# Storing one of eight expert results between two pieces of the last weight load

## The chip, the cores and the metric

The kernel runs on one core of a Trainium2 chip. A core has TensorE for matmuls, VectorE and ScalarE for elementwise work, GpSimd and SyncE, and 16 DMA engines that move data between the chip's memory (HBM) and the on-chip memory (SBUF). Engines run side by side and wait for one another through semaphores. A transfer is issued by one of the engines into its queue; the 16 DMA engines then serve the queues, and the transfer raises a semaphore by 16 when all of it has landed. The metric is the device time of one execution in microseconds (us).

## The reference

Eight experts, each with two layers and a ReLU between them:

```python
# x: [8, 256, 512], w1: [8, 512, 2048], w2: [8, 2048, 512], float32
h = np.matmul(x, w1)
h = np.maximum(h, 0)
return np.matmul(h, w2).astype(np.float32)     # [8, 256, 512]
```

Per expert 512 KB of x, 4 MB of w1 and 4 MB of w2 come in, and 512 KB of result go out. All the weights are read once: 64 MB in float32.

## The kernel before

**Where the data lies.** Weights are converted to bf16 by the transfer that loads them, so 4 MB in HBM become 2 MB in SBUF. There are two buffers for w1 and two for w2; expert e uses buffer e % 2. The results have a place for every expert: `o_sb` holds all eight, `[128, 8, 2, 512]` in float32, and nothing in it is overwritten.

**The computation.** Experts go in pairs, four rounds of a loop. In each round TensorE runs layer 1 of both experts (L255 to L275, 64 matmuls per expert into `ph`), while VectorE and ScalarE apply the ReLU and write `ht` (L215, L217). Then it runs layer 2 of both (L277 to L296). One expert's layer 2 is 16 contraction tiles times two halves of the rows, 32 matmuls into one PSUM tile `po`, which VectorE and ScalarE copy to `o_sb`, one half each (L224). Each copy raises a counter by one: `s_dve` for VectorE, `s_act` for ScalarE. The helper `copied(eng, n)` (L100) makes an engine wait for both counters, so for the results of the first n experts.

**What sets the order of the loads.** All weights are loaded through GpSimd's queue, in an order written out by hand (L139 to L162): the w1 of a pair, then its w2, each held back until the buffer that it fills is free. The w2 load of the last two experts is cut into two transfers, the first 9 contraction tiles (1152 KB, L136) and the other 7 (896 KB, L137), so that the pass can begin on the first piece. TensorE does not wait for loads directly: SyncE waits for each load's semaphore in turn and hands TensorE a token (`t_w`, L105 to L121). For the last expert TensorE takes one token before contraction tile 0 and one before tile 9 (L285). Before the first of them, SyncE also waits until the previous expert's result has been copied out of `po` (L116).

**The stores.** There are three before the change. GpSimd issues one for results 0 to 3 at the end of its program, after the last weight transfer (L163, L164). SyncE issues one for results 4 to 6, after it has seen the last weight piece land and result 6 copied (L122, L123), and one for result 7 when that has been copied (L124, L125). At the end SyncE waits for the three store semaphores (L298, L299).

Of the kernel before, what the change touches and what calls it, by code (L numbers as in the profile page):

```python
# [9 lines left out]
def kernel(  # L10
# [13 lines left out]
    E, C, H = x.shape  # L24
# [6 lines left out]
    G = E // 2  # L31
# [5 lines left out]
    out_r = out.rearrange("e (p mt) n -> p e mt n", p=P)  # L37
# [18 lines left out]
    o_sb = nc.alloc_sbuf_tensor("out_sb", [P, E, MT, H], f32)  # L56
# [8 lines left out]
    s_out = [sem(f"s_out{i}") for i in range(3)]  # L65
# [18 lines left out]
    sp, pool, act, dve, pe = nc.sync, nc.gpsimd, nc.scalar, nc.vector, nc.tensor  # L84
# [15 lines left out]
    def copied(eng, n):  # L100
        eng.wait_ge(s_act, n)
        eng.wait_ge(s_dve, n)
# [28 lines left out]
    def load_w2(e):  # L131
        k = e % 2 * KT2
        if e < E - 2:
            pool.dma_start(w2_k[:, k:k + KT2], w2_r[e]).then_inc(s_w2[e], 16)  # L134
        else:
            pool.dma_start(w2_k[:, k:k + CUT], w2_r[e, :, :CUT]).then_inc(s_w2[e], 16)  # L136
            pool.dma_start(w2_k[:, k + CUT:k + KT2], w2_r[e, :, CUT:]).then_inc(s_w2b[e - E], 16)  # L137

    load_x(pool, G - 1, 1, 2)  # L139
# [12 lines left out]
        channel_multiplier=1,  # L152
    ).then_inc(s_id, 1)
    load_w2(0)
    load_w2(1)
    for e in range(2, E, 2):
        for b in range(2):
            pool.wait_ge(s_first, e + b - 1)
            load_w1(e + b)
        for b in range(2):  # L160
            pool.wait_ge(s_act, e + b - 1)
            load_w2(e + b)  # L162
    copied(pool, G)  # L163
    pool.dma_start(out_r[:, :G], o_sb[:, :G]).then_inc(s_out[0], 16)  # L164
    pool.drain()


# [127 lines left out]
                    if kt == KT2 - 1:  # L295
                        ins.then_inc((s_ob, s_oa)[m], 1)  # L296

    for s in s_out:  # L298
        sp.wait_ge(s, 16)  # L299


# [28 lines left out]
```

## Time and profile before

| What | Value |
|---|---|
| Median of 3 runs | 179.64 us (179.51 to 179.72) |
| The profiled execution: time | 179.63 us |
| The profiled execution: span from first to last instruction | 178.3 us |
| TensorE busy | 134.0 us, 75% |
| VectorE, ScalarE busy | 37.1 us, 37.8 us |
| HBM read, written | 71.30 MB, 4.19 MB |
| Mean granted TensorE clock | 0.943 |

The times quoted below are in microseconds from the start of the span. In the page's slices, each digit is a tenth of the busy share of one of 40 equal slices (9 is 90% or more), and the GB/s row counts the bytes that the transfers wrote. "Landing" is the moment at which a transfer's semaphore is complete; a row of the transfers gives the size of one and the time from issue to landing. In rows of the timeline the columns are start, duration, engine, line, operation and operands, and in brackets the idle time before it with what ended it. "SPq" is SyncE's queue of instructions.

### The profile page before, as it was taken

The page shows a single profiled execution, that of the slowest core. Times are in us where ns is not written, and L with a number is a line of the kernel's source. Part 1 is how long each engine was busy: PE and PEld are TensorE (multiplying, and loading weights), DVE is VectorE, ACT ScalarE, POOL GpSimd, SP SyncE. Part 2 cuts the span into 40 slices and gives each one's busy share as a digit, 9 for nine tenths or more (in the row PEclk, how much of TensorE's full clock was granted, in tenths as well). Part 3 has the DMA queues.
Part 4 walks back from the last instruction along what each step waited for, and adds up shares of the span by engine and source line. Part 5 has one row for each costly group of instructions (what it writes and reads, how often), then busy time and mean ns, then how long its engine had stood idle before and what let it go on. Part 6 is the DMA issues. An engine that isn't in the chain of part 4 may idle for free. (4 is left out here: it accounts for less than half of the span.)

```text
span 178.3 us, 2361 instructions
## 1 busy us (share of the span) xinstructions
PE 134.0 (75%) x832; PEld 90.8 (51%) x832; DVE 37.1 (21%) x48; ACT 37.8 (21%) x49; POOL 12.9 (7%) x27
## 2 busy tenths in 40 slices
PE   0044479899949697899769399999499695998950
PEld 0033368796414296785233278874134694953420
DVE  0132653342010133131101023330100242311010
ACT  2455555222010122121100013230100221311010
POOL 3600000101010101001000100110200400000000
PEclk9999999999987999699999759999969999999996
DMA  6999999999999999999998999999999999999998
GB/s 210 347 211 232 232 199 217 232 206 210 235 202 210 235 210 202 235 210 202 235 221 191 235 221 195 232 232 199 217 232 202 213 235 190 214 217 210 269 422 359
DMA packets 4368, 40.90 MB, mean 229 GB/s; under 512 B 400, under 2 KB 400, under 8 KB 2192
## 3 DMA queue, kind: packets, MB, share of 16 engines
q0 software_dynamic: 3408, 37.23, 95.1%
q1 hardware_dynamic: 960, 3.67, 5.3%
HBM read 71.30 MB, written 4.19 MB: 423 GB/s over the span
## 5 line engine op out<-in xcount | busy, mean ns | idle before, releaser
L268 PE MATMUL pt_h<-xe,w_sb 128*128 x512 | 67.3, 291 | 11.2 <-PEq L87 11.1
L268 PEld LDWEIGHTS pt_h<-xe,w_sb 128*128 x512 | 58.8, 148 | 20.2 <-issue 17.1
L288 PE MATMUL pt_o<-w_sb,ht_sb 128*128 x256 | 59.9, 395 | 8.9 <-PEq L87 8.8
L288 PEld LDWEIGHTS pt_o<-w_sb,ht_sb 128*128 x256 | 25.5, 101 | 41.8 <-issue 15.6
L217 DVE TENSOR_SCALAR ht_sb<-pt_h 128x512 bf16<-128x512 f32 x32 | 22.1, 692 | 52.3 <-PE pt_h L268 52.3
L215 ACT ACTIVATE ht_sb<-pt_h 128x512 bf16<-128x512 f32 x32 | 19.1, 597 | 57.3 <-PE pt_h L268 57.3
L252 PE MATMUL pt_tr<-identity,x_b 128*128 128x128 bf16 x64 | 7.5, 308 | 17.8 <-PEq L87 17.8
L224 DVE COPY out_sb<-pt_o 128x512 f32 x8 | 5.5, 692 | 65.4 <-PE pt_o L288 65.4
L224 ACT COPY out_sb<-pt_o 128x512 f32 x8 | 4.7, 585 | 63.6 <-PE pt_o L288 63.6
L252 PEld LDWEIGHTS pt_tr<-identity,x_b 128*128 128x128 bf16 x64 | 6.5, 142 | 18.5 <-issue 18.5
L129 POOL DMA_DIRECT2D w_sb<-in_w_dram x8 | 5.0, 625 | 73.3 <-ACTq L219 73.3
L194 DVE COPY xe<-pt_tr 128x1024 bf16<-128x1024 bf16 x2 | 4.9, 2460 | 5.2 <-PE pt_tr L252 5.2
L194 ACT COPY xe<-pt_tr 128x1024 bf16<-128x1024 bf16 x2 | 4.9, 2455 | 4.1 <-PE pt_tr L252 4.1
L134 POOL DMA_DIRECT2D w_sb<-in_w_dram x6 | 3.2, 536 | 34.0 <-ACT out_sb L224 33.9
L175 ACT CAST x_b<-x_f 128x1024 bf16<-128x1024 f32 x2 | 4.0, 1986 | 3.2 <-DMA x_f<-in_x_dram 3.2
L191 DVE COPY xe<-pt_tr 128x1024 bf16<-128x1024 bf16 x2 | 1.4, 692 | 8.1 <-PE pt_tr L252 8.1
L175 DVE CAST x_b<-x_f 128x1024 bf16<-128x1024 f32 x2 | 2.1, 1060 | 4.2 <-DMA x_f<-in_x_dram 4.2
L191 ACT COPY xe<-pt_tr 128x1024 bf16<-128x1024 bf16 x2 | 2.0, 1012 | 4.1 <-PE pt_tr L252 4.1
L136 POOL DMA_DIRECT2D w_sb<-in_w_dram x2 | 1.1, 528 | 17.6 <-ACT out_sb L224 17.6
L175 ACT COPY x_b<-x_c 128x1024 bf16<-128x1024 bf16 x2 | 2.2, 1122 | 0.0
L175 ACT ACT_TABLE_LOAD x1 | 1.3, 1283 | 2.5 <-PEq L98 2.5
L175 DVE COPY x_b<-x_c 128x1024 bf16<-128x1024 bf16 x2 | 1.4, 698 | 0.0
(10 smaller groups left out, 4.0 us busy)
## 6 DMA issues: line engine op xcount, KB each, us to landing
w_sb<-in_w_dram POOLq DMA_DIRECT2D x14, 2048.0 KB, 28.8
w_sb<-in_w_dram POOLq DMA_DIRECT2D x2, 1152.0 KB, 25.5
out_dram<-out_sb POOLq DMA_DIRECT2D x1, 2048.0 KB, 34.0
w_sb<-in_w_dram POOLq DMA_DIRECT2D x2, 896.0 KB, 29.4
out_dram<-out_sb SPq DMA_DIRECT2D x1, 1536.0 KB, 8.6
x_f<-in_x_dram SPq DMA_DIRECT2D x1, 1024.0 KB, 5.7
x_c<-in_x_dram POOLq DMA_DIRECT2D x1, 1024.0 KB, 9.4
x_f<-in_x_dram SPq DMA_DIRECT2D x1, 512.0 KB, 3.4
```

The costliest lines, as they stand in the source:

```text
L129: pool.dma_start(w1_k[:, e % 2 * KT1:(e % 2 + 1) * KT1], w1_r[e]).then_inc(s_w1[e], 16)
L134: pool.dma_start(w2_k[:, k:k + KT2], w2_r[e]).then_inc(s_w2[e], 16)
L136: pool.dma_start(w2_k[:, k:k + CUT], w2_r[e, :, :CUT]).then_inc(s_w2[e], 16)
L175: copy(x_b[:, b].rearrange("p (t m) q -> p t m q", m=MT), src.rearrange("p m (q t) -> p t m q", t=KT1),).then_inc(t_xb, 1)
L191: copy(xe[:, a * n:(a + 1) * n], pt[b][:].rearrange("p j q -> p (j q)")).then_inc(s_xe[b], 1)
L194: copy(xl[:, :, :, :, a - G].rearrange("p l j q -> p j l q"), pt[b][:].rearrange("p j (l q) -> p j l q", l=G),).then_inc(s_xe[b], 1)
L215: act.activation(dst, ph[half][:], relu).then_inc(t_h, 1)
L217: dve.tensor_relu(dst, ph[half][:]).then_inc(t_h, 1)
L224: copy(outs[b], po[:, half]).then_inc(s_copied, 1)
L252: ins = pe.transpose(pt[b][:, j], x_b[:, b, j], identity[:])
L268: ins = pe.matmul(ph[i // 2][:, i % 2, :], ws[i % 2 * KT1 + kt], xs[kt], start=(kt == 0), stop=(kt == KT1 - 1),)
L288: ins = pe.matmul(po[:, m], hs[(kt - k0) * MT + m], ws[kt - k0], start=(kt == 0), stop=(kt == KT2 - 1),)
```

## The change

GpSimd issues the store of result 0 as a transfer of its own, 512 KB, after the first piece of expert 7's w2 and before the second. Ahead of it stands a wait for result 0's two copies. The store at the end of GpSimd's program now covers results 1 to 3, 1536 KB. Both raise the same semaphore, so SyncE's last wait asks for 32 on it instead of 16. Nothing else is changed.

```diff
@@ load_w2 @@
             pool.dma_start(w2_k[:, k:k + CUT], w2_r[e, :, :CUT]).then_inc(s_w2[e], 16)
+            if e == E - 1:
+                copied(pool, 1)
+                pool.dma_start(out_r[:, 0], o_sb[:, 0]).then_inc(s_out[0], 16)
             pool.dma_start(w2_k[:, k + CUT:k + KT2], w2_r[e, :, CUT:]).then_inc(s_w2b[e - E], 16)
@@ end of GpSimd's program @@
     copied(pool, G)
-    pool.dma_start(out_r[:, :G], o_sb[:, :G]).then_inc(s_out[0], 16)
+    pool.dma_start(out_r[:, 1:G], o_sb[:, 1:G]).then_inc(s_out[0], 16)
     pool.drain()
@@ SyncE's last waits @@
-    for s in s_out:
-        sp.wait_ge(s, 16)
+    for i, s in enumerate(s_out):
+        sp.wait_ge(s, 16 if i else 32)
```

## The prediction

> **What bounds the kernel now.** I read the slices of the page first, then the transfers and their landings, then the waits of SyncE, then the end of the span in small windows.
>
> ```profile
> span 178.3 us, 2361 instructions
> DMA  6999999999999999999998999999999999999998
> GB/s 210 347 211 232 232 199 217 232 206 210 235 202 210 235 210 202 235 210 202 235 221 191 235 221 195 232 232 199 217 232 202 213 235 190 214 217 210 269 422 359
> q0 software_dynamic: 3408, 37.23, 95.1%
> q1 hardware_dynamic: 960, 3.67, 5.3%
> PE 4%; ACT 0%; issue 0%
> ```
>
> The DMA row stands at 9 tenths in nearly every slice, the last ones included. The chain that ended last holds only 4% of TensorE, its last layer-2 pass; what comes after it is a transfer. The kernel is bound by bytes through the 16 DMA engines, and nearly all go through GpSimd's queue (q0, 95.1%). The rate of the row doubles at the end, from about 215 to 422 GB/s, because it counts bytes written: a weight load reads float32 and writes bf16, a store writes what it reads.
>
> Which transfer ends last, by issue time and time to landing:
>
> ```profile
> 139.11 0.53 POOL L136 DMA_DIRECT2D w_sb<-in_w_dram  x1 [10.39 <-ACT out_sb L224]
> 139.63 0.54 POOL L137 DMA_DIRECT2D w_sb<-in_w_dram  x1
> 140.15 0.76 POOL L164 DMA_DIRECT2D out_dram<-out_sb  x1
> 168.37 0.39 SPq L123 DMA_DIRECT2D out_dram<-out_sb  x1
> 172.51 0.36 SPq L125 DMA_DIRECT2D out_dram<-out_sb  x1
> ...
> w_sb<-in_w_dram POOLq DMA_DIRECT2D x1, 1152.0 KB, 24.7
> w_sb<-in_w_dram POOLq DMA_DIRECT2D x1, 896.0 KB, 28.6
> out_dram<-out_sb POOLq DMA_DIRECT2D x1, 2048.0 KB, 34.0
> out_dram<-out_sb SPq DMA_DIRECT2D x1, 1536.0 KB, 8.6
> out_dram<-out_sb SPq DMA_DIRECT2D x1, 512.0 KB, 5.7
> ```
>
> Adding the two times: the first piece of expert 7's w2 lands at 139.11 + 24.7 = 163.8, the second at 139.63 + 28.6 = 168.2, the store of results 0 to 3 at 140.15 + 34.0 = 174.2, that of 4 to 6 at 168.37 + 8.6 = 177.0 and that of 7 at 172.51 + 5.7 = 178.2. The last landing is the end of the span. GpSimd's three land in the order of issue and were all issued over 20 us before they could move, so its queue is one line, long filled ahead.
>
> The end in windows. Columns: stretch, its length, busy time of PE, PEld, DVE, ACT and POOL, granted clock, DMA share, GB/s.
>
> ```profile
> 163.00:168.23 5.23, 4.44 (x21) 1.87 (x20) 0.69 (x1) 0.58 (x1) 0.00 (x0) 1.00 1.01 217
> 168.23:177.50 9.27, 3.63 (x17) 1.47 (x15) 0.69 (x1) 0.58 (x1) 0.00 (x0) 0.87 1.02 422
> 176.00:176.50 0.50, 0.00 (x0) 0.00 (x0) 0.00 (x0) 0.00 (x0) 0.00 (x0) 0.50 1.02 418
> 176.50:177.00 0.50, 0.00 (x0) 0.00 (x0) 0.00 (x0) 0.00 (x0) 0.00 (x0) 0.50 1.02 418
> 177.50:178.00 0.50, 0.00 (x0) 0.00 (x0) 0.00 (x0) 0.00 (x0) 0.00 (x0) 0.50 0.28 107
> ```
>
> From 163 to 177.5 the engines have a share of 1: no gap between the two w2 pieces, between load and store, or where SyncE's queue alone is left (176 to 177). The bytes that remain after the second piece are 8 results of 512 KB, 4.194 MB, and 4.194 MB / 422 GB/s = 9.94 us; 168.23 + 9.94 = 178.17 against the landing at 178.2. So the end is the landing of the second w2 piece plus the stores at full rate.
>
> **The change part by part.** The sum is made against the profiled execution: 178.3 us of span, 179.63 us with what lies around it, 0.01 under the median of the runs, 179.64.
>
> Result 0 on its own. The 2048 KB store becomes one of 512 KB ahead of the second w2 piece and one of 1536 KB behind it. No byte is added. The 512 KB take 0.524 MB / 422 GB/s = 1.24 us of all engines before the second piece, and as much less after it. For the DMA engines: +1.24 and −1.24, sum 0. GpSimd issues one transfer more, 0.53 us by the row of L136, and the second piece is issued some 0.6 us later, at about 140.2. That costs nothing, since its turn on the engines comes only after 163; without that cover it would be 0.6 us.
>
> The new wait on GpSimd, for expert 0's two output copies. Behind it stand the second piece and the other store. It is already met:
>
> ```profile
> L224 DVE COPY out_sb<-pt_o x8: 691/692/692, 49.2 to 171.7; 128x512 f32 x8
> L224 ACT COPY out_sb<-pt_o x8: 585/585/586, 49.4 to 171.9; 128x512 f32 x8
> ```
>
> The first copies start at 49.2 and 49.4 and take 0.7 and 0.6 us, so both counts are there by 50, and GpSimd comes to the wait at about 139.6, after the issue of the first piece. Cost 0.
>
> The second w2 piece lands 1.24 us later, at 168.23 + 1.24 = 169.47. TensorE waits for it before its contraction tile 9 of 16, that is after 18 of 32 matmuls:
>
> ```profile
> SPq L121 <- DMA w_sb<-in_w_dram: 3.6, 1, 3.6
> L121 SPq EVENT_SEMAPHORE  x2: 17/17/17, 158.4 to 168.2; - x2
> 164.80 7.07 PE L288 MATMUL pt_o<-w_sb,ht_sb 128*128 x32 [0.79 <-PEq L87]
> 171.69 0.69 DVE L224 COPY out_sb<-pt_o 128x512 f32 x1 [7.16 <-PE pt_o L288]
> 171.90 0.58 ACT L224 COPY out_sb<-pt_o 128x512 f32 x1 [7.27 <-PE pt_o L288]
> ```
>
> SyncE passes that wait at 168.2 and hands the token on. TensorE reaches tile 9 at 164.80 + 18 x 7.07 / 32 = 168.78 and does not stop: the pass is one run of 32. The slack is 0.5 us, and the delay of 1.24 us uses it up. I expect a new stall of 1.24 − 0.5 = 0.7 us, 0.9 if SyncE's handing-on takes 0.2. The copies then end at 172.48 + 0.8 = 173.3, and the store of result 7 is issued at 173.4 instead of 172.51.
>
> What is queued behind SyncE's wait: the store of results 4 to 6. It goes from 168.37 to about 169.6, as it is issued once the second piece has landed.
>
> Does the late issue reach the end? Only if the engines run out of work first. From 169.47 there are 7 results left, 3.670 MB / 422 GB/s = 8.70 us, up to 178.17, as before. Without result 7 the others keep the engines until 178.17 − 1.24 = 176.9 by landings, and some 0.6 us earlier, 176.3, by the last byte (the data of the profiled run end in the window 177.5 to 178 at 0.28 x 0.5 = 0.14, so at 177.64, against the landing at 178.2). A transfer started from rest needs this long to its first bytes:
>
> ```profile
> 0.74 0.87 SPq L92 DMA_DIRECT2D x_f<-in_x_dram  x2
> 1.00:1.50 0.50, 0.00 (x0) 0.00 (x0) 0.00 (x0) 0.00 (x0) 0.00 (x0) 1.00 0.00 0
> 1.50:2.00 0.50, 0.00 (x0) 0.00 (x0) 0.00 (x0) 0.00 (x0) 0.00 (x0) 1.00 0.65 90
> ```
>
> Issue at 0.74, first bytes between 1.5 and 2: about 1.0 us, at most 1.3. So the store of result 7 is in time if it is issued by about 175.2; it comes at 173.4. The stall of 0.8 us is covered by 1.8 us. The first store of SyncE has the same cover: it must be ready before GpSimd's 1536 KB are through, at 169.47 − 0.6 + 1.573 MB / 422 GB/s = 172.6, and is, at 169.6 + 1.0 = 170.6. Cost of both on the path: 0. What is late next, were the stall longer, is the issue of result 7.
>
> The engines now go from load to store, back to load, and to store again. The change from load to store costs nothing that the share shows (1.01 and 1.02 on either side). The change from a store back to a load is in no row. Nearest rows: a transfer behind another on the same queue, 0, from the share of 1.02 in 176 to 177, where SyncE's second store follows its first; and a start from rest, 1.0 us. GpSimd's queue is filled ahead, which makes it the first of the two: I take 0.05 us, and keep 0 and 1.0. Below nothing it goes if the store slips in beside the load, which writes only 217 GB/s: at most the 1.24 us of the store.
>
> A term of this one execution lies in the same place:
>
> ```profile
> 165.00:165.50 0.50, 0.50 (x4) 0.25 (x3) 0.00 (x0) 0.00 (x0) 0.00 (x0) 1.00 1.19 229
> 165.50:166.00 0.50, 0.50 (x4) 0.24 (x3) 0.00 (x0) 0.00 (x0) 0.00 (x0) 1.00 1.18 172
> 166.00:166.50 0.50, 0.50 (x4) 0.20 (x2) 0.00 (x0) 0.00 (x0) 0.00 (x0) 1.00 0.70 115
> 166.50:167.00 0.50, 0.50 (x4) 0.24 (x3) 0.00 (x0) 0.00 (x0) 0.00 (x0) 1.00 0.93 186
> ```
>
> The load falls from 217 to 172, 115 and 186 GB/s for half a microsecond each, (45 + 102 + 31) x 0.5 = 89 KB, at 217 GB/s 0.4 us, from no cause that I see. If it does not come again the time falls by up to 0.4; if a store there makes it worse, it grows by as much.
>
> Sum: +1.24 − 1.24 + 0 (issue) + 0 (wait) + 0 (stall, covered) + 0.05 = +0.05, on 179.64: 179.7.
>
> **The rivals.** *Slower: the ring stands still between a store and what follows it.* If the completion mark of result 0's store holds GpSimd's queue until its last byte is confirmed in memory, the engines idle, for SyncE's queue is empty then. The price is the time from last byte to landing at the end, 178.2 − 177.64 = 0.57: 180.2. Against it stands the seamless pass from SyncE's first store to its second, 1.02; for it, that this is another queue, and that no store of GpSimd's has anything behind it yet. A read that starts cold after the store would cost about the same or up to 1.0.
>
> *Slower: a transfer more pays a whole start and end.* The rows give 1.0 for a start and 0.57 for an end: 1.57, 181.2. Against it: the two w2 pieces are two transfers already, 4.4 us apart for 896 KB, and show no hole in the share. The Trainium skill, "DMA: Bandwidth & Descriptors", section "Anatomy of one DMA — SWDGE (gpsimd) path", states a fit of about 2.0 us per transfer plus its bytes at 436 GB/s. Read as a charge on every transfer, it speaks against cutting a store in two, and the sum by it would be an estimated 181.6; the trace bears the rate out (422) and not the charge for transfers that are queued back to back.
>
> *Slower: the stall reaches the end.* This decides only if the result 7 store is issued after 175.2, the second piece landing past 171.3 in place of 169.47. It needs 1.8 us more than 512 KB cost; one more microsecond beyond that gives 180.6. GpSimd's queue would have to be served out of order, which its three landings deny.
>
> *Faster: the store hides under the load.* A load occupies half of the write side (217 against 422 GB/s). If the engines used the rest, all of result 0's 1.24 us would vanish: 178.4; a half, 179.0; the dip at 165.5 to 167 not coming again, 179.2. Against the first: the share is 1.0 in loads already, and an engine that must read 4 bytes for each 2 written has no reading side left for a store.
>
> **How the numbers follow.** Faster or slower means over 0.2%, 0.36 us, about what a measurement here tells from no change. Bytes conserved, no gap: 0.60, 179.7, its own range 179.3 to 180.0. The ring stands still or reads start cold, 180.2 to 180.6: 0.18. A full start and end: 0.06. The stall reaches the end: 0.04. Faster by overlap or by the missing dip: 0.12, mostly at 179.0 to 179.2. So faster 0.12, same 0.60, slower 0.28. The range 179.2 to 180.6 leaves out the full charge, the long stall and most of the overlap, under 2 in 10.
>
> **What would show it.** Right: the second piece lands about 1.2 us later, near 169.5; the last layer-2 pass splits into 18 and 14 matmuls with 0.7 to 0.9 us between; SyncE's stores go out near 169.6 and 173.4; the DMA share stays at 1 from 163 to 177.5; the last landing stays at 178.2. Wrong: a half-microsecond window between 163 and 170 with a share well under 1 that the trace of before does not have (the ring stands still, or the cold read); a hole after 176 (the late issue); a second piece that lands less than 0.8 us later (overlap).

## The result, and the profile after

The changed kernel takes 179.88 us against 179.59 us (medians of 20 executions each): a ratio of 1.0015 with a 95% interval of 1.0009 to 1.0022. It is slower by about 0.27 us, clearly above nothing and, at 0.15%, inside the 0.2% that was called no change, though the upper end of the interval lies just outside. It also spreads more. The executions of before lie between 179.51 and 179.91, those of the changed kernel between 179.56 and 180.55, leaving out a single one of 340.15.

The profiled execution took 179.56 us with a span of 178.2. GpSimd's and SyncE's issues in its timeline:

```profile
139.16 0.53 POOL L136 DMA_DIRECT2D w_sb<-in_w_dram  x1 [10.38 <-ACT out_sb L227]
139.71 0.54 POOL L139 DMA_DIRECT2D out_dram<-out_sb  x1
140.24 0.54 POOL L140 DMA_DIRECT2D w_sb<-in_w_dram  x1
140.77 0.76 POOL L167 DMA_DIRECT2D out_dram<-out_sb  x1
169.58 0.39 SPq L123 DMA_DIRECT2D out_dram<-out_sb  x1
173.44 0.36 SPq L125 DMA_DIRECT2D out_dram<-out_sb  x1
```

The transfers of the same execution, by size and time from issue to landing:

```profile
w_sb<-in_w_dram POOLq DMA_DIRECT2D x1, 1152.0 KB, 24.8
out_dram<-out_sb POOLq DMA_DIRECT2D x1, 512.0 KB, 25.6
w_sb<-in_w_dram POOLq DMA_DIRECT2D x1, 896.0 KB, 29.2
out_dram<-out_sb POOLq DMA_DIRECT2D x1, 1536.0 KB, 32.5
out_dram<-out_sb SPq DMA_DIRECT2D x1, 1536.0 KB, 7.4
out_dram<-out_sb SPq DMA_DIRECT2D x1, 512.0 KB, 4.8
```

The first piece lands at 139.16 + 24.8 = 164.0, result 0 at 165.3, the second piece at 140.24 + 29.2 = 169.44, results 1 to 3 at 173.3, 4 to 6 at 177.0 and 7 at 178.2. In this execution the order of the landings has changed and the end has not.

TensorE's last pass in the timeline:

```profile
164.84 3.83 PE L291 MATMUL pt_o<-w_sb,ht_sb 128*128 x17 [0.79 <-PEq L87]
169.61 3.18 PE L291 MATMUL pt_o<-w_sb,ht_sb 128*128 x14 [0.93 <-PEq L87]
```

The pass of 32 is now two runs with a stall of 0.93 us (one matmul record is missing). The DMA engines over the whole stretch, in the columns of the windows shown before:

```profile
163.00:177.50 14.50, 8.06 (x36) 3.28 (x35) 1.38 (x2) 1.17 (x2) 0.00 (x0) 1.00 1.00 350
```

The share is 1.00, where the same window of before has 1.02, and the span is 178.2 us against 178.3. So this execution shows no loss against before, and the 0.27 us of the medians must lie in others.

### The profile page after: what moved, and what is told of

It reads as the page before. It is cut to its first block, busy times and chain, and to the rows that moved or that the text cites. A ratio compares the mean times of both kernels' runs of the same rounds, so it can differ in the third digit from the quotient of the medians.

```text
span 178.2 us, 2355 instructions
## 1 busy us (share of the span) xinstructions
PE 129.4 (73%) x824; PEld 88.0 (49%) x832; DVE 37.1 (21%) x48; ACT 37.8 (21%) x49; POOL 13.4 (7%) x28
## 5 line engine op out<-in xcount | busy, mean ns | idle before, releaser
L271 PE MATMUL pt_h<-xe,w_sb 128*128 x512 | 63.2, 278 | 12.7 <-PEq L87 12.7
L291 PE MATMUL pt_o<-w_sb,ht_sb 128*128 x248 | 59.1, 394 | 13.1 <-PEq L87 12.7
L271 PEld LDWEIGHTS pt_h<-xe,w_sb 128*128 x512 | 56.3, 146 | 20.2 <-issue 19.4
```

The lines of the kernel that those rows point to most:

```text
L271: ins = pe.matmul(ph[i // 2][:, i % 2, :], ws[i % 2 * KT1 + kt], xs[kt], start=(kt == 0), stop=(kt == KT1 - 1),)
L291: ins = pe.matmul(po[:, m], hs[(kt - k0) * MT + m], ws[kt - k0], start=(kt == 0), stop=(kt == KT2 - 1),)
```

## The experiments

Theory 1 at the start: bytes are conserved and the stall is covered; the 0.27 us comes from executions that spread. Its rival: a fixed cost of the added transfer or of the added change between load and store.

### The changed kernel, profiled twice more

No edit.

> The changed kernel once more, unaltered, with its profile. It was 0.15% (0.27 us) slower than before, though its profiled execution of 179.56 us shows every byte and every stall where the prediction had them. Theory 1 (bytes conserved, stall covered, the 0.27 us comes from executions that spread): again 179.55 to 180.5 us from run to run, with a median 0.1 to 0.5 us above before, and in a profile of a longer execution a place between 163 and 178 us where the transfer engines stand still or the packets run slow. Rival (a fixed cost of the added transfer or of the added change of direction): a constant +0.25 us in every execution, visible as a share under 1 near 164.7 or 168.7 us in any profile.

> The changed kernel a third time for its profile. Theory 2: the DMA rate dips in the first piece of w2 shortly before 163 us, and in some executions also in the second piece, ahead of 168.7; the end of the span lies the later, the later the second piece lands (169.44 with a span of 178.2, 169.9 with 178.7). Rival: the landing is the same and the end differs.

With five rounds it took 179.88 us against 179.63, a ratio of 1.0014 (1.0005 to 1.0023). The two profiled executions took 179.98 and 179.81 us, with spans of 178.7 and 178.5. The second piece among the transfers of the one of 178.7, and of the one of 178.5:

```profile
w_sb<-in_w_dram POOLq DMA_DIRECT2D x1, 896.0 KB, 29.7
```

```profile
w_sb<-in_w_dram POOLq DMA_DIRECT2D x1, 896.0 KB, 31.2
```

Issued at 140.17 and 138.45, it lands at 169.87 and 169.65, against 169.44 in the execution of 178.2. Adding the 8.70 us that seven results take at 422 GB/s gives 178.57, 178.35 and 178.14, for spans of 178.7, 178.5 and 178.2. So what differs between executions happens before that landing; the stores behind it go at the same rate. A fixed cost of 0.27 us in every execution does not fit the first profile, whose span is not longer than that of before, nor the executions of 179.56 to 179.64 us in the first comparison, since the fastest of before there plus 0.27 is 179.78.

### Split without the move

```diff
-    pool.dma_start(out_r[:, :G], o_sb[:, :G]).then_inc(s_out[0], 16)
+    pool.dma_start(out_r[:, 0], o_sb[:, 0]).then_inc(s_out[0], 16)
+    pool.dma_start(out_r[:, 1:G], o_sb[:, 1:G]).then_inc(s_out[0], 16)
```

> Result 0 is stored by a transfer of its own, but behind both pieces of expert 7's w2, directly ahead of the store of results 1 to 3. Theory 1: the second piece lands at 168.2 as before, no stall, the time of before within 0.1 us, with no more spread than before. Rival (the extra transfer is charged): +0.27 us or more, as in the changed kernel; by the full charge of the prediction's rival +1.6 us.

179.65 us against 179.63, ratio 0.9999 (0.9990 to 1.0008). A transfer more, behind the loads, costs nothing that is measured. The charge of a whole start and end, 1.57 us, the prediction's second rival, is excluded, here and by the 0.27 us of the changed kernel.

### More results ahead of the second piece

```diff
             if e == E - 1:
-                copied(pool, 1)
-                pool.dma_start(out_r[:, 0], o_sb[:, 0]).then_inc(s_out[0], 16)
+                copied(pool, 2)                      # 4 in the other kernel
+                pool.dma_start(out_r[:, :2], o_sb[:, :2]).then_inc(s_out[0], 16)
```

> Results 0 and 1 (1024 KB) are stored ahead of the second piece, 2 and 3 behind it. Theory 1: the second piece lands 2 x 1.24 us later than before, at 170.7; TensorE stalls about 2.2 us; SyncE's stores are issued at 170.8 and 174.7, the last one 0.5 us before the limit of 175.2, so the end stays at 178.2 and the median within 0.5 us of before. Rival (TensorE's stall goes to the end): +1.3 us over the changed kernel. Rival (a cost per change of direction, not per byte): the same 0.27 us as the changed kernel.

> Results 0 to 3 (2048 KB) are all stored ahead of the second piece, none behind it. Theory 1: the second piece lands 4 x 1.24 us later, at 173.2; SyncE's first store is issued at 173.3 and starts at 174.3, while GpSimd's queue has been empty since 172.6, so the engines stand still for 1.7 us; the last store is issued at 177.2 and starts at 178.2, a further 0.2 us late; the span ends near 180.1, +1.9 us or 1.1%. Rival (bytes alone decide, SyncE's stores start at once): +0.3 us at most. Rival (the whole stall of TensorE of 4.6 us shows): +4.6 us.

The kernel with four ahead stores results 0 to 3 ahead of the piece, so no store stands behind it in GpSimd's queue. Two ahead: 180.64 us, 1.0053 (1.0031 to 1.0075). Four ahead: 183.49 us, 1.0220 (1.0194 to 1.0245), about 3.9 us where 1.9 was expected. Both were missed. The last pass and the last store in the timeline with two ahead, and then the windows after the stall:

```profile
164.96 4.04 PE L291 MATMUL pt_o<-w_sb,ht_sb 128*128 x18 [0.79 <-PEq L87]
171.69 4.87 PE L291 MATMUL pt_o<-w_sb,ht_sb 128*128 x14 [2.69 <-PEq L87]
...
177.21 0.36 SPq L125 DMA_DIRECT2D out_dram<-out_sb  x1
```

```profile
173.00:174.00 1.00, 1.00 (x3) 0.30 (x2) 0.00 (x0) 0.00 (x0) 0.00 (x0) 0.50 1.01 414
174.00:175.00 1.00, 1.00 (x4) 0.38 (x3) 0.00 (x0) 0.00 (x0) 0.00 (x0) 0.50 1.04 426
176.50:177.00 0.50, 0.06 (x1) 0.00 (x0) 0.50 (x1) 0.40 (x1) 0.00 (x0) 1.00 0.55 221
177.00:177.50 0.50, 0.00 (x0) 0.00 (x0) 0.07 (x1) 0.18 (x1) 0.00 (x0) 1.00 0.17 66
177.50:178.00 0.50, 0.00 (x0) 0.00 (x0) 0.00 (x0) 0.00 (x0) 0.00 (x0) 1.00 0.00 0
```

TensorE goes on at 171.69 after a stall of 2.69 us. About 1 us later, in the window from 172.5 to 173 (mean 0.73), the granted clock falls to 0.50, and the last 14 matmuls take 4.87 us in place of 3.18. SyncE's first store is also later than expected, 171.66 in place of 170.8. Together this puts the store of result 7 at 177.21 (174.7 expected), beyond the prediction's limit of 175.2, and the engines run dry: a share of 0.17 and then 0 up to 178. With four ahead the same two things are larger, in the timeline and the windows:

```profile
173.60 4.71 PE L289 MATMUL pt_o<-w_sb,ht_sb 128*128 x14 [4.78 <-PEq L87]
...
178.96 0.36 SPq L125 DMA_DIRECT2D out_dram<-out_sb  x1
```

```profile
173.00:173.50 0.50, 0.00 (x0) 0.00 (x0) 0.00 (x0) 0.00 (x0) 0.00 (x0) 0.82 0.01 0
173.50:174.00 0.50, 0.40 (x2) 0.16 (x3) 0.00 (x0) 0.00 (x0) 0.00 (x0) 0.50 0.00 0
178.50:179.00 0.50, 0.00 (x0) 0.00 (x0) 0.33 (x1) 0.43 (x1) 0.00 (x0) 1.00 0.00 0
```

The first hole, up to 174.5, was expected, because SyncE's first store is issued only at 173.57. The second, at 178.5, comes from the late store of result 7, and that mostly from the slower clock: 4.71 − 3.18 = 1.5 us, where the span of this execution, 181.7 us, is 1.6 us over the expected 180.1. (It was the fastest of the four executions; the rest of what the median missed is not explained.) So the limit of the prediction is real, and a long stall can bring a second cost with it. In the changed kernel the stalls were 0.93, 1.16 and 1.00 us in the three profiles, the 14 matmuls took 3.18 us in each, and the clock stayed at 1.00. The Trainium skill, "TensorE: Matmul & The Clock Gate", Part 1, gives an idle window of about 3.4 us for the fall to half the clock; here the fall followed a pause of 2.69 us. That is no threshold. Another pause in the same execution with two ahead, just as long, was followed by a pass at the full clock:

```profile
129.59 7.07 PE L291 MATMUL pt_o<-w_sb,ht_sb 128*128 x32 [2.69 <-PEq L87]
```

In the kernel before, a pause of 2.66 us ahead of the pass at 90.70 changed nothing (7.07 us for 32 matmuls), while one of 1.91 us ahead of 71.90 was followed by a fall between 72.5 and 73 and a pass of 9.24 us in place of 7.77. So pauses of about 2 to 3 us are sometimes followed by half the clock and sometimes not, and that the stall brought it about here is likely and not shown.

### No store behind the second piece; the kernel before once more

```diff
-    pool.dma_start(out_r[:, :G], o_sb[:, :G]).then_inc(s_out[0], 16)
...
-    for s in s_out:
+    for s in s_out[1:]:
```

> The kernel before without the store of results 0 to 3, which are left out of the output; nothing stands behind the second w2 piece in GpSimd's queue. Theory 2 (a load runs slower in its last microseconds when a store follows it in the same queue, and each such place adds some tenths of a microsecond): the dip of the kernel before between 165.5 and 167 us is gone, the load stays near 217 to 229 GB/s to its end, and the second piece lands about 0.3 us sooner, 28.3 us after its issue in place of 28.6. Rival (the dip has a cause of its own, unrelated to the store): it is there again, at the same place.

> The kernel before once more, for a second profile of it. Theories 2 and 3: the second w2 piece loses 0.2 to 0.4 us again, near 165 to 167 us, and no other load of the run does. Rival (a chance event of the first profile): no dip, or one elsewhere.

The edit leaves the store of results 0 to 3 out, and with it these results. The windows below are the last 1.5 us in which all engines still load the second piece. First the kernel before, first and second profile:

```profile
165.50:167.00 1.50, 1.50 (x9) 0.68 (x8) 0.00 (x0) 0.00 (x0) 0.00 (x0) 1.00 0.94 158
```

```profile
165.50:167.00 1.50, 0.73 (x4) 0.40 (x5) 0.49 (x1) 0.58 (x1) 0.00 (x0) 1.00 1.06 205
```

Then the split without the move, and the kernel with no store behind the piece:

```profile
165.50:167.00 1.50, 1.50 (x9) 0.68 (x7) 0.00 (x0) 0.00 (x0) 0.00 (x0) 1.00 1.05 177
```

```profile
165.50:167.00 1.50, 0.80 (x4) 0.42 (x5) 0.42 (x1) 0.53 (x1) 0.00 (x0) 1.00 1.08 225
```

With a store behind it the load runs at 158, 205 and 177 GB/s, without one at 225. The share stays near 1 in all of them, so packets are slower and the engines are not idle. A window of 1.5 us counts the packets that start in it, so its rate also depends on where its edges fall; the share divided by the rate does not, and it goes with the time of one packet. By it a packet takes 24%, 8% and 24% longer with the store (0.94 / 158 against 1.08 / 225, and so on). The packet records of the same traces agree: without the store each of the 128 packets of the piece takes 549 ns, with it they take 589, 563 and 588 on average. The dip that the prediction could not explain is tied to the store, and its size changes from run to run.

SyncE's first store, issued as soon as the piece has landed, goes out at 168.37, 168.29 and 168.41 with the store and at 168.08 without. Of this 0.2 to 0.3 us, 0.1 to 0.2 us belong to the dip: the piece's first packet already started 0.13 to 0.18 us later in the three.

The second profile of before shows something else. TensorE's last pass began 1.5 us later there, at 166.27, and the store of result 7 was issued at 173.99 in place of 172.51, yet the span is 178.2. That is the prediction's cover at work, in the kernel before.

### Result 0 ahead of the first piece

```diff
+            if e == E - 1:
+                copied(pool, 1)
+                pool.dma_start(out_r[:, 0], o_sb[:, 0]).then_inc(s_out[0], 16)
             pool.dma_start(w2_k[:, k:k + CUT], w2_r[e, :, :CUT]).then_inc(s_w2[e], 16)
```

> Result 0 is stored ahead of the first piece of expert 7's w2 in place of between the two. As many changes between load and store as in the changed kernel, but TensorE no longer stops in the middle of the pass: the first piece lands at 163.8 + 1.24 = 165.0, the pass starts 0.4 us late and stops about 0.5 us at tile 9. Theory 2: a median 0.15 to 0.3 us above before, like the changed kernel. Rival (the place between the two pieces, or the stop at tile 9, is what costs): the time of before within 0.1 us.

179.86 us against 179.56, ratio 1.0027 (1.0016 to 1.0037). TensorE's stall at tile 9 was 0.21 us and the store of result 7 went out at 173.65, inside the limit, so it is not that stall which costs. The load ahead of the store is now expert 6's second piece. In a window of it, the kernel before and this one:

```profile
154.50:158.00 3.50, 3.50 (x28) 2.72 (x26) 1.21 (x2) 1.19 (x2) 0.00 (x0) 1.00 1.06 220
```

```profile
154.50:158.00 3.50, 3.50 (x28) 2.73 (x26) 1.21 (x2) 1.19 (x2) 0.00 (x0) 1.00 0.99 178
```

220 and 178 GB/s, and by share over rate packets that are 15% longer: the dip has moved with the store. In the changed kernel it sits at the end of the first piece. A window there, in the kernel before and then in the three profiles of the changed kernel in the order 178.2, 178.7 and 178.5:

```profile
160.60:163.10 2.50, 2.50 (x13) 1.18 (x12) 0.00 (x0) 0.00 (x0) 0.00 (x0) 1.00 1.01 212
```

```profile
160.60:163.10 2.50, 2.45 (x12) 1.15 (x12) 0.00 (x0) 0.00 (x0) 0.00 (x0) 1.00 1.00 192
```

```profile
160.60:163.10 2.50, 2.50 (x13) 1.17 (x12) 0.00 (x0) 0.00 (x0) 0.00 (x0) 1.00 1.04 184
```

```profile
160.60:163.10 2.50, 2.50 (x13) 1.18 (x12) 0.00 (x0) 0.00 (x0) 0.00 (x0) 1.00 1.02 181
```

The rates alone do not show it, since this window reads 199 and 206 GB/s in the second profile of before and with no store. Share over rate does: it is about the same as in before for those two (0.95 / 199 and 0.99 / 206 against 1.01 / 212), and 9%, 19% and 18% more in the changed kernel. That is 2.5 x (1 − 1 / 1.09) = 0.2 us lost, 0.4 and 0.4. By the packet records the first piece's packets take 728, 751 and 750 ns on average, and 700 in both profiles of before. The second piece, with results 1 to 3 behind it, has no dip in the first and third of them (229 and 225 GB/s in 165.5 to 167) and a slight one in the second (210).

### Result 0 in quarters

```diff
+    def store_quarter(i):
+        if i == 0:
+            copied(pool, 1)
+        r = slice(32 * i, 32 * i + 32)
+        pool.dma_start(out_r[r, 0], o_sb[r, 0]).then_inc(s_out[0], 16)
...
+            store_quarter(2 * (e - E + 2))
             pool.dma_start(w2_k[:, k:k + CUT], w2_r[e, :, :CUT]).then_inc(s_w2[e], 16)
+            store_quarter(2 * (e - E + 2) + 1)
             pool.dma_start(w2_k[:, k + CUT:k + KT2], w2_r[e, :, CUT:]).then_inc(s_w2b[e - E], 16)
```

> Result 0 is stored in four quarters of 32 partitions (128 KB each), ahead of each of the four w2 pieces of experts 6 and 7: as many bytes ahead of the last piece as in the changed kernel, the stall at tile 9 again near 0.9 us, but five changes from load to store in place of two. Theory 2: about 0.2 us for each change more, so +0.6 us over the changed kernel, 180.3 to 180.6. Rival (bytes alone, and a cost that does not go by the number of changes): as the changed kernel, +0.27 us over before. A small fixed charge for each of three more transfers is not told apart from theory 2 by the time, but by the place: slow load packets against a pause.

179.50 us against 179.56, ratio 1.0006 (0.9988 to 1.0025; one execution of 181.47 widens it). That is no loss, with as many bytes ahead of the last piece as in the changed kernel, a stall of 0.52 us and three more changes between load and store. Theory 2, a cost for each change from load to store, falls. Theory 3, to be tried next: it is the load ahead of the first store that slows down, and a small first store costs little.

### One quarter alone, in three places

```diff
+            if e == E - 2:                           # quarter_early; E - 1 and behind the first piece: quarter_mid
+                copied(pool, 1)
+                pool.dma_start(out_r[:32, 0], o_sb[:32, 0]).then_inc(s_out[0], 16)
...
-    pool.dma_start(out_r[:, :G], o_sb[:, :G]).then_inc(s_out[0], 16)
+    pool.dma_start(out_r[32:, 0], o_sb[32:, 0]).then_inc(s_out[0], 16)
+    pool.dma_start(out_r[:, 1:G], o_sb[:, 1:G]).then_inc(s_out[0], 16)
```

> The kernel before, but the first quarter of result 0 (32 partitions, 128 KB) is stored ahead of the first w2 piece of expert 6, by GpSimd; its other three quarters and results 1 to 3 follow behind the last piece. Theory 3 (it is the load ahead of the first store of the run that slows down, not every load ahead of a store; a small first store costs little): the last w2 piece runs at full rate although a store follows it, lands 0.31 (the quarter) - 0.3 (the dip that is gone) = 0.0 us from before, and the end comes 0.1 to 0.3 us sooner: 179.3 to 179.5 us. Theory 2 (every load ahead of a store slows down): the dip near 166 us is there as before, and the time is that of before or 0.1 us more.

> The same quarter at the place of the change, between the two pieces of expert 7's w2; everything else of results 0 to 3 behind. The second piece lands 0.31 us later than before, inside the slack of 0.5 us, so there is no stall. Theory 3: a dip in the first piece as large as a small first store makes it (0.1 us by the quarters), full rate in the second: 179.4 to 179.6 us. Theory 2: two dips, 179.7 to 179.9 us. Rival (the place between the pieces costs by itself): +0.27 us like the changed kernel.

> The same quarter is stored by SyncE's queue in the second round of experts, near 85 us, with a semaphore of its own; the rest of results 0 to 3 stays behind the last w2 piece in GpSimd's queue. If it is the first store at all that slows the loads around it (theory 3a): no dip near 166 us, 179.3 to 179.5 us. If it is the first store in GpSimd's queue (theory 3b) or any store there (theory 2): the dip is there, 179.5 to 179.7 us.

Against 179.58 us they took 179.48 (ratio 0.9994, 0.9985 to 1.0003), 179.47 (0.9993, 0.9984 to 1.0002) and 179.62 (1.0003, 0.9994 to 1.0012). The window at the end of the second piece, in this order:

```profile
165.50:167.00 1.50, 0.71 (x5) 0.35 (x5) 0.55 (x1) 0.59 (x1) 0.00 (x0) 1.00 1.03 215
```

```profile
165.50:167.00 1.50, 1.50 (x8) 0.69 (x7) 0.00 (x0) 0.00 (x0) 0.00 (x0) 1.00 1.04 201
```

```profile
165.50:167.00 1.50, 1.50 (x9) 0.68 (x7) 0.00 (x0) 0.00 (x0) 0.00 (x0) 1.00 1.03 191
```

With the early quarter in GpSimd's queue there is no dip there (215, and 549 ns for the packets of the piece), though a store follows; with the quarter on SyncE's queue there is one (191, 577 ns); the one in the middle lies between (201, 563 ns). So a first store elsewhere doesn't help. Theory 3 is not borne out either. With the early quarter SyncE's first store went out at 168.75, 0.4 us later than in before, where no delay was expected: the slow packets now stand ahead of the quarter, in expert 7's w1 (1250 ns in place of 1227). With the quarter in the middle the dip is in the second piece, which theory 3 had at full rate, and not in the first (700 ns). And with two results ahead the second piece is slowed more than the first (624 ns in place of 549, 710 in place of 700), though its store is not the first.

The early and the middle quarter are 0.1 us under before, which their intervals don't tell from nothing; no kernel here is shown to be faster than the kernel before. What they do show: at the very place of the change 128 KB cost nothing that is measured, and 512 KB cost 0.27 us.

How far the slow packets account for the times can be added up from the packet records: what the weight packets take beyond 549, 700 and 1227 ns (second pieces, first pieces, whole loads), over the 16 engines.

| Kernel | Lost to slow packets, us per profile | Median against before, us |
|---|---|---|
| no store behind the piece | 0 | not comparable |
| before (two profiles), split alone | 0.32, 0.18, 0.31 | 0, +0.02 |
| changed (three profiles) | 0.28, 0.52, 0.48 | +0.27 |
| result 0 ahead of the first piece | 0.49 | +0.30 |
| quarters; early, middle, SyncE's | 0.18; 0.25, 0.12, 0.25 | −0.06; −0.10, −0.11, +0.04 |

From before and split to changed the mean grows by 0.16 us, and the mean time of the same profiled executions by 0.17. So slow load packets account for the difference between the profiled executions; of the 0.27 us between the medians, 0.1 us is left open, with three profiles on each side.

## Why the prediction was right, and what it mis-sized

Right, by its steps:

- *The bytes.* The second piece lands at 169.44 in the first profile (169.47 foretold), and the stores behind it still end at 178.2. That the two agree to 0.03 us is luck: the other two profiles have 169.87 and 169.65.
- *The wait.* GpSimd issues the next transfers 0.5 us apart, with no pause for the counters.
- *The stall.* 0.93, 1.16 and 1.00 us, against 0.7 to 0.9.
- *The cover.* SyncE's stores go out at 169.58 and 173.44 in that profile (169.6 and 173.4 foretold), and the engines stay filled to the end. The limit of 175.2 was tried from both sides, if not closely: 173.99 costs nothing, 177.21 empties the engines.
- *No charge for another transfer.* Split alone, the ratio is 0.9999.

Mis-sized: the cost of the engines' changes between load and store. The prediction took 0.05 us, and looked for it in the passage from the store back to the load. It had read the passage from load to store as free, because the DMA share is 1.01 and 1.02 on either side. That reading failed: the share stays at 1 while the rate falls. The dip that it put down as a term of one execution, from no cause that it saw, was this cost, already paid once in the kernel before (0.1 to 0.3 us in the second piece by the packet records). The prediction did leave room for a store that makes it worse. The change moves it to the first piece and makes it larger there in two of three profiles. The second piece lands 1.21, 1.64 and 1.42 us later than in the first profile of before in place of 1.24, a mean of 1.42: 0.18 us over the term, on medians that differ by 0.27.

Two readings were off without bearing on the result. The last bytes of before move until 177.9 (123 GB/s in 177.7 to 177.8), not 177.64, so the time from the last byte to the landing is about 0.3 us and not 0.57; this puts the limit near 175.5 and the first rival's price at 0.3. And by the packet records the first piece starts to move at 157.5, 18.4 us after its issue, not over 20.

Not settled: why a load slows down ahead of a store in its queue, and why a store of 512 KB ahead of a weight piece costs more than one of 128 KB, while the store of 1536 KB behind the second piece of the changed kernel slows that piece little or not at all. The numbers for the dip come from one to three profiles per kernel, and it also varies between executions of the same kernel. The longest executions of the changed kernel, 180.2 to 180.55 us, were not profiled, so whether they have a larger dip, or a fall of the clock after the stall, is open.

## What to carry to other kernels

Where the transfer engines are full to the end, the order of the transfers moves waits and, but for some tenths of a microsecond, not the end, until a late issue leaves the engines without work: work out that limit and compare the new issue time with it. Read the rate beside the busy share, since a slow packet counts as busy, and divide the two for the time of a packet. And ask how long the new stall is: one of about 1 us cost nothing here, and one of 2.7 us was followed by half the matmul clock.

## What the runs showed of the hardware

- A weight load that stands ahead of a store in GpSimd's queue can run slower in its last microseconds: 158 to 205 GB/s written in place of 225, with the share of busy engines near 1 and packets of 563 to 589 ns on average in place of 549. It moved when the store moved (178 in place of 220 for expert 6's second piece) and was gone in the one profile without the store. Not every load ahead of a store slows down: the last piece of the kernel with quarters kept 549 ns.
- Pauses of TensorE of 0.93 to 1.16 us left the granted clock at 1.00. After pauses of 1.91 to 2.69 us it fell to 0.50 in some places (4.87 us for 14 matmuls in place of 3.18) and stayed at 1.00 in others.
